# Second expert products in plain float32, all remaining expert splits on VectorE, and another order of the first transfers, in a decoder layer with conv, attention, state-space and 16 experts

## The chip, the core and the metric

The kernel runs on one core of a Trainium2 chip. A core has five engines with in-order instruction streams of their own: TensorE (PE; its weight loads are shown as PEld), VectorE (DVE), ScalarE (ACT), GpSimd (POOL) and SyncE (SP), which here only issues transfers. They meet through semaphores. The metric is the device time of one launch in microseconds (us).

## The reference

One layer over 1040 tokens (16 learned meta tokens and 1024 tokens of x) with a model width of 1024, all in float32. After the layer the meta rows are dropped.

```python
z = rms_norm(h, norm_mix_g)
cv_a, cv_g, q, k, v, f_lg, s_u = split(z @ w_in)
y = concat(conv(cv_a, cv_g),               # depthwise, 31 taps, layer norm, silu
           rms_norm(attention(q, k, v, f_lg)),
           rms_norm(s5_mixer(s_u, lam_re, lam_im, log_dt, ...)))   # 32 groups x 64 states
h = h + y @ w_out
t = rms_norm(h, norm_ffn_g)
# router: best of 4 groups, best 2 of its 4 experts -> gates[:, 16]
for e in range(16):
    out += gates[:, e:e+1] * ((silu(t @ w1[e]) * (t @ w3[e])) @ w2[e])   # 1024 -> 256 -> 1024
h = h + out
return rms_norm(h, final_norm_g)[16:]
```

`ssm_lam_re` and `ssm_lam_im` have shape (32, 64) and `ssm_log_dt` has shape (32): one number for each group and state, and one for each group.

## The kernel before, in words

**Split products.** Most matrix products are made of three TensorE passes in the type fp32r. An operand is split into a high part (ScalarE copies it into fp32r) and a low part (the rest, by a subtraction on VectorE or GpSimd). `mm3` (L283 to L289) then adds high times high (L287), high times low (L288) and low times high (L289) for each 128 rows of the contraction. A float32 operand that goes into a matmul unsplit is multiplied in plain float32; one pair of products of the state-space part does that already (L1946).

**Front.** Nine token tiles (the meta rows and eight of 128 tokens, called x0 to x7 here) are requested by `load_h` on SP into `hb`, which has three buffers. `norm_h` takes the mean square on ACT (L315), scales the tile on DVE (L320), turns it with eight TensorE transposes (L326), and splits it (ACT L328 high, DVE L329 low). `load_w` requests 128 columns of `w_in` (L344) and splits them (L346, L347). The first three column groups are multiplied chunk by chunk (400, 384 and 256 tokens): I call these chunks c0, c1 and c2. Each has three groups of 24 matmuls, so c0 to c2 are 216 matmuls. They need tiles meta to x2, x3 to x5, and x6 and x7.

**State-space parameters.** `ssm_tables.params` (L1638 on) reads lam_re, lam_im (L1675, L1676) and log_dt (L1678) straight into the layout of 128 partitions x 8, so that each element is a piece of a transfer by itself. A chain of small DVE instructions makes exponentials, sines and cosines from them. `build` makes tables on GpSimd and DVE: the W tables (1024 elements a partition, L1631 to L1636), and E by repeated doubling on GpSimd (8 to 512 elements wide). `kernel` turns W on TensorE (L1824) and multiplies it (L1831).

**Order of the work.** Up to the experts a scheduler orders the instructions of each engine at build time. In the expert part the order is written out by hand: a list ORDER of step names is walked once for each expert `e` (with `e - 1` and `e + 1` overlapped).

**Experts.** For each expert the rows routed to it come in one or two blocks of 128 tokens, gathered by GpSimd (L1239). The second block hangs on a branch. A block is turned on TensorE (L1249), split (ACT L1255, DVE L1256), multiplied with w1 and w3 (`first`: 8 x 3 matmuls of 512 columns), gated (ACT L1266, DVE L1268, L1269), turned again (L1275), split (`gate_turned`: ACT L1280, DVE L1281), and multiplied with w2 (`second`: for each of two halves 2 x 3 matmuls of 512 columns). The result is scaled by the gate and added to the rows in memory by an indirect transfer (L1292). The weights of an expert are three loads (`load`) of 128 x 2048 floats: q = 0 and 1 hold w1 and w3, q = 2 holds w2. Each is split in two halves by `split`: one ACT copy (L1327) and one subtraction (L1328) of 128x1024 each. The steps a0, a1, b0, b1 (q = 0, 1) give the subtraction to VectorE, the steps w0, w1 (q = 2) to GpSimd (VectorE for the last expert). The loads share six buffers `eraw`, and their high and low parts five buffers each. After the last gather, rows of the residual are read, added, normed and written out beside the last experts (`residuals`, `dense_in`, `dense_out`, `tick`). A loop for a third and later block of an expert stands behind it and is not entered with these inputs.

## Time and profile before

| | |
|---|---|
| time, median of 3 runs | 943.05 us (940.55 to 946.97) |
| the profiled execution's own time, and its span | 945.53 us, 943.8 us |
| mean granted TensorE clock in it (1 is full speed) | 0.916 |
| TensorE matmuls | 795.9 us busy, 84% of the span |
| VectorE | 723.5 us, 77% |
| ScalarE | 464.0 us, 49% |
| GpSimd | 415.7 us, 44% |
| transfers | 122.13 MB, 135 GB/s of main memory traffic over the span |

The busy tenths in 40 slices of 23.6 us say where an engine is full. TensorE starts at 0 and 5, has 9 in most slices up to the experts, 6 to 9 in the experts (slices 27 to 38) and 0 in the last. VectorE has 9 in the slices of the convolution and of the tail. A row of a view of groups gives the line, the engine, the operation, the tiles and shapes, the count, the busy time and the mean of one instruction, and then how long the engine stood idle just before such an instruction and what ended that. Because the engines work in order, an instruction that waits holds up all that stands behind it on its engine.

### The profile page before, as it was taken

Reading aid. Unit: us, or ns where it says so; the run is one execution under the profiler, and the core shown is the slowest. Engines: PE = TensorE matmul, PEld = TensorE weight load, DVE = VectorE, ACT = ScalarE, POOL = GpSimd, SP = SyncE. Lnnn points to the kernel's source line nnn. Section 1 sums busy time; section 2 is a strip of 40 time slices with the busy share of each in tenths; the row PEclk is TensorE's granted clock in tenths of the full one; section 3 lists DMA queues with packets and bytes.
Section 4 is the critical chain, followed back from the end, with each engine's and each line's share of the span. In section 5 each row is a group of like instructions: output and inputs, shape, how many; then the busy total and the mean of one; then the engine's idle time right before and its main releaser. Section 6 shows DMA issues by size and latency. Waiting matters only on the chain. (4 is left out here: it accounts for less than half of the span.)

```text
span 943.8 us, 15100 instructions
## 1 busy us (share of the span) xinstructions
PE 795.9 (84%) x5154; PEld 661.4 (70%) x5155; DVE 723.5 (77%) x1712; ACT 464.0 (49%) x803; POOL 415.7 (44%) x437
## 2 busy tenths in 40 slices
PE   0588898899999978989989999927899997998680
PEld 0488897698999956666668888825687775776560
DVE  3853997988858488998977657675779688798895
ACT  3332265325234275776764332415557476577662
POOL 0094995740000063656683001143456456456465
PEclk9999998899999986998978999958999999998795
DMA  5513125113220032011124341119788779879652
GB/s 124 158 46 93 39 63 114 31 26 101 53 90 24 1 113 79 24 69 40 43 100 139 112 134 68 67 46 351 264 269 263 247 195 276 263 219 295 234 205 98
DMA packets 92084, 122.13 MB, mean 129 GB/s; under 512 B 17931, under 2 KB 72986, under 8 KB 92000
## 3 DMA queue, kind: packets, MB, share of 16 engines
q1 hardware_dynamic: 84944, 101.98, 33.2%
q0 software_dynamic: 7056, 19.09, 7.9%
q8 instruction: 45, 0.74, 0.3%
q14 instruction: 39, 0.32, 0.1%
HBM read 101.16 MB, written 26.52 MB: 135 GB/s over the span
## 5 line engine op out<-in xcount | busy, mean ns | idle before, releaser
L287 PE MATMUL psum<-arena,arena 128*128 128x512 f32 (+5 forms) x848 | 309.2, 365 | 12.1 <-ACT arena L513 4.1
L288 PE MATMUL psum<-arena,arena 128*128 128x512 f32 (+5 forms) x848 | 303.1, 358 | 7.3 <-DVE arena L347 4.3
L289 PE MATMUL psum<-arena,arena 128*128 128x512 f32 (+5 forms) x848 | 302.0, 357 | 0.0
L287 PEld LDWEIGHTS psum<-arena,arena 128*128 128x128 f32 (+1 forms) x848 | 164.1, 194 | 33.7 <-issue 7.2
L288 PEld LDWEIGHTS psum<-arena,arena 128*128 128x128 f32 (+1 forms) x848 | 164.1, 194 | 23.5 <-DVE arena L347 4.5
L289 PEld LDWEIGHTS psum<-arena,arena 128*128 128x128 f32 (+1 forms) x848 | 163.5, 193 | 17.0 <-DVE arena L347 0.4
L1328 POOL TENSOR_TENSOR arena<-arena,arena 128x1024 fp32r<-128x1024 f32 x34 | 90.7, 2672 | 106.1 <-ACT arena L1327 90.4
L773 POOL TENSOR_TENSOR arena<-arena 128x512 f16<-128x512 f32 (+4 forms) x104 | 109.0, 1066 | 62.5 <-DVE arena L772 36.0
L1328 DVE TENSOR_TENSOR arena<-arena,arena 128x1024 fp32r<-128x1024 f32 x62 | 121.5, 1992 | 18.8 <-ACT arena L1327 18.7
L1327 ACT ACTIVATE arena<-arena 128x1024 fp32r<-128x1024 f32 x96 | 98.7, 1072 | 4.0 <-DMA arena<-in_exp_w_dram 2.9
L767 ACT ACTIVATE arena<-psum,arena 128x512 f32<-128x512 f32 (+4 forms) x112 | 63.8, 588 | 36.8 <-PE psum L763 15.9
L670 DVE CUSTOM_DVE_ANT_0 arena<-psum,arena 128x144 bf16<-128x144 f32 (+6 forms) x112 | 54.9, 501 | 22.3 <-PE psum L665 9.0
L1249 PE MATMUL psum<-arena 128*128 128x128 f32 x256 | 43.7, 302 | 32.3 <-DVE arena L1256 23.2
L780 PE MATMUL psum<-arena,arena 128*128 128x65 f16 (+3 forms) x1056 | 61.5, 206 | 7.9 <-DVE arena L741 3.4
L780 PEld LDWEIGHTS <-arena 128*128 128x128 f16 (+1 forms) x1056 | 47.8, 105 | 28.7 <-POOL arena L773 10.4
L1249 PEld LDWEIGHTS psum<-arena 128*128 128x128 f32 x256 | 33.1, 154 | 46.8 <-DVE arena L1256 28.7
L1255 ACT ACTIVATE arena<-psum 128x512 fp32r<-128x512 f32 x64 | 38.5, 601 | 43.1 <-PE psum L1249 43.1
L759 PE MATMUL psum<-arena 128*128 128x512 f32 (+4 forms) x112 | 52.3, 468 | 1.7 <-ACT arena L770 1.2
L665 PE MATMUL psum<-arena 128*128 128x144 f32 (+7 forms) x112 | 45.4, 411 | 7.9 <-DVE arena L670 7.8
L433 DVE SCALAR_TENSOR_TENSOR psum<-arena,psum 128x1024 f32<-128x1024 f32 x40 | 51.3, 1282 | 0.7
L819 POOL MEMSET arena<- 128x9 f16 x2 | 0.2, 166 | 115.6 <-PE psum L288 115.6
L443 POOL TENSOR_TENSOR arena<-arena 128x512 f32<-128x512 f32 x36 | 48.6, 1377 | 5.7 <-ACT arena L440 5.7
(315 smaller groups left out, 1479.4 us busy)
## 6 DMA issues: line engine op xcount, KB each, us to landing
arena<-in_exp_w_dram SPq DMA_DIRECT2D x64, 512.0 KB, 7.5
arena<-in_exp_w_dram SPq DMA_DIRECT2D x16, 1024.0 KB, 5.3
arena<-in_x_dram SPq DMA_DIRECT2D x16, 512.0 KB, 4.5
arena<-in_w_in_dram SPq DMA_DIRECT2D x14, 512.0 KB, 4.3
arena<-cr_d SPq DMA_DIRECT2D x8, 520.0 KB, 3.7
arena<-in_w_out_dram SPq DMA_DIRECT2D x8, 512.0 KB, 3.6
h_d<-arena SPq DMA_DIRECT2D x8, 512.0 KB, 3.0
t_d<-arena SPq DMA_DIRECT2D x8, 512.0 KB, 4.0
```

The source lines that it names most:

```text
L287: PE.matmul(out=acc, lhsT=lh[k], rhs=rh[k], start=(k == 0), stop=False)
L288: PE.matmul(out=acc, lhsT=lh[k], rhs=rl[k], start=False, stop=False)
L289: PE.matmul(out=acc, lhsT=ll[k], rhs=rh[k], start=False, stop=(k == n - 1))
L433: V.scalar_tensor_tensor(out=yc, in0=ub[:, m, w:w + NX], scalar=cwt[:, m, w:w + 1], in1=yc, op0=OP.mult, op1=OP.add)
L670: V.tensor_tensor_reduce(out=jk_b()[:, :b - a], in0=sp, in1=nrow[:, a:b], scale=1.0, scalar=-3.0e38, op0=OP.add, op1=OP.max, accum_out=mp[ ...
L759: PE.matmul(out=sp, lhsT=KS[:, k0:k0 + nk], rhs=QS[:, q0:q1], start=True, stop=False)
L767: S.activation(out=pt, in_=sp, func=AF.Exp, bias=bias)
L773: (V if cnt[0] % 5 in HV[h] else G).tensor_tensor(out=pl, in0=pt, in1=ph, op=OP.subtract)
L780: PE.matmul(out=po[:, i - i0, 0:v1 - v0], lhsT=w[:, qs], rhs=vb[:nk, j, v0:v1], start=(j == 0 and i == i0 and n == 0), stop=(j == i and n ...
L1249: PE.transpose(tp[:, k, :], xg[:, c:c + 128], ident)
L1327: S.activation(out=h[:, cs], in_=raw[:, cs], func=AF.Copy)
L1328: eng.tensor_tensor(out=l[:, cs], in0=raw[:, cs], in1=h[:, cs].bitcast(F32), op=OP.subtract)
```

## The change

- All nine token tiles get a buffer of their own (`hb` 9), and all are requested near the start of the program.
- lam_re, lam_im and log_dt are read as rows (8 partitions x 128, and 8 x 2), log_dt is repeated over 64 states by a DVE copy, three TensorE transposes turn them, and one DVE copy brings them from PSUM into place.
- `gate_turned` only copies (ACT), and `second` multiplies plain float32 operands: two matmuls for each half and no low parts. w2 is not split any more: the steps w0 and w1 are gone. w2 gets three buffers of its own (`ew2`), and its load for expert e + 3 is requested behind the second product of expert e. `eraw` goes from six to four buffers, and the high and low parts from five to four.

```diff
+    par = A.alloc("par", [3, 128], parts=8), A.alloc("par2", [2], parts=8)
-    hb = A.rot("h", [D], 3)
+    hb = A.rot("h", [D], 9)
...
     load_h(2)
+    load_h(3)
     norm_h(0, 2)
     wu = [load_w(2056, 128)]
-    load_h(3)
+    load_h(4)
     norm_h(2, 3)
     wu.append(load_w(2056 + 128, 128))
-    load_h(4)
+    load_h(5)
     norm_h(3, 4)
     wu.append(load_w(256, 128))
+    for i in range(6, 9):
+        load_h(i)
...
         if c == 0:
             for i in range(5, 8):
-                load_h(i)
                 norm_h(i - 1, i)
         if c == 1:
-            load_h(8)
...
-        raw = raw_b()
+        raw = raw_b() if q < 2 else w2_b()
...
-        order += [(e + 1, 1)] * (e + 1 < NE) + [(e, 2)] + [(e + 2, 0)] * (e + 2 < NE)
+        order += [(e + 1, 1)] * (e + 1 < NE) + [(e + 2, 0)] * (e + 2 < NE)
...
-    raw_b.more(3)
+    raw_b.more(1)
-    wh_b = A.rot("ewh", [2048], 5, F32R)
-    wl_b = A.rot("ewl", [2048], 5, F32R)
+    wh_b = A.rot("ewh", [2048], 4, F32R)
+    wl_b = A.rot("ewl", [2048], 4, F32R)
+    w2_b = A.rot("ew2", [2048], 3, flex=False)
...
     def gate_turned(tp):
-        ah, al = ah_b(), al_b()
-        S.activation(out=ah, in_=tp, func=AF.Copy, scale=0.5)
-        V.scalar_tensor_tensor(out=al, in0=tp, scalar=0.5, in1=ah.bitcast(F32), op0=OP.mult,
-                               op1=OP.subtract)
-        return ah, al
+        aa = aa_b()
+        S.activation(out=aa, in_=tp, func=AF.Copy, scale=0.5)
+        return aa
...
-        mm3(yp, [ah[:, k, :] for k in range(2)], [al[:, k, :] for k in range(2)],
-            [w2[0][:, k, cs] for k in range(2)], [w2[1][:, k, cs] for k in range(2)])
+        for k in range(2):
+            PE.matmul(out=yp, lhsT=aa[:, k, :], rhs=w2[:, k, hf * 512:hf * 512 + 512],
+                      start=(k == 0), stop=(k == 1))
...
+    def load2(e):
+        if e < NE:
+            w2s[e] = v2(load_raw(e, 2))
...
             for k in ([hf] if b == 0 else range(2)):
                 second(w2s[e], aa[e, b], yps[e, b, k], k)
+        if b:
+            load2(e + 3)
...
-        "w0": (lambda e: split(e, 2, 0, G if e + 1 < NE else V), 0),
-        "w1": (lambda e: split(e, 2, 1, G if e + 1 < NE else V), 0),
...
+        SY.dma_start(out=pr[:, 0, :], in_=dram(p["ssm_lam_re"], 0, [[128, 8], [1, 128]]))
+        SY.dma_start(out=pr[:, 1, :], in_=dram(p["ssm_lam_im"], 0, [[128, 8], [1, 128]]))
+        SY.dma_start(out=l2, in_=dram(p["ssm_log_dt"], 0, [[2, 8], [1, 2]]))
+        V.tensor_copy(out=pr[:, 2, :].rearrange("q (a s) -> q a s", a=2),
+                      in_=l2[:, :, None].to_broadcast([8, 2, 64]))
+        tp = self.bank("ss")[:, :24].rearrange("p (k q) -> p k q", q=8)
+        for k in range(3):
+            PE.transpose(tp[:, k, :], pr[:, k, :], self.ident[:8, :8])
         lr, li, ld = t8(), t8(), t8()
-        SY.dma_start(out=lr, in_=dram(p["ssm_lam_re"], 0, [[1, 128], [128, 8]]))
-        SY.dma_start(out=li, in_=dram(p["ssm_lam_im"], 0, [[1, 128], [128, 8]]))
-        for par in range(2):
-            SY.dma_start(out=ld[par * 64:par * 64 + 64], in_=dram(p["ssm_log_dt"], par, [[0, 64], [2, 8]]))
+        V.tensor_copy(out=self.sm[:, self.cnt - 3:self.cnt, :], in_=tp)
```

The change adds lines, so a line of the front stands at 1 to 4 higher numbers in the changed kernel, and one of the tables at 3 to 9 higher. Three places of the order that the diff alone does not tell follow.

First place: SP, whose transfers go out in this order, from its first weight load on. Before:

```order
L344 DMA arena_61<-in_w_in_dram 128x8x128 x2
L1675 DMA arena_61<-in_ssm_lam_re_dram 128x8x1
L1676 DMA arena_61<-in_ssm_lam_im_dram 128x8x1
L1678 DMA arena_61<-in_ssm_log_dt_dram 64x8x1 x2
L1681 DMA arena_61<-in_ssm_b_re_dram 128x8x16
L1681 DMA arena_61<-in_ssm_b_im_dram 128x8x16
L1926 DMA arena_865<-in_ssm_norm_g_dram 128x256
L310 DMA arena_61<-in_x_dram 128x1024
L344 DMA arena_61<-in_w_in_dram 128x8x128 x2
L310 DMA arena_61<-in_x_dram 128x1024
L344 DMA arena_61<-in_w_in_dram 128x8x128
L310 DMA arena_61<-in_x_dram 128x1024 x3
```

Of the change:

```order
L345 DMA arena_61<-in_w_in_dram 128x8x128
L311 DMA arena_61<-in_x_dram 128x1024
L345 DMA arena_61<-in_w_in_dram 128x8x128
L311 DMA arena_61<-in_x_dram 128x1024 x4
L413 DMA arena_61<-in_conv_w_dram 31x256
L416 DMA arena_61<-in_conv_b_dram 128x2x1
L1678 DMA arena_61<-in_ssm_lam_re_dram 8x128
L1679 DMA arena_61<-in_ssm_lam_im_dram 8x128
L1680 DMA arena_61<-in_ssm_log_dt_dram 8x2
L1690 DMA arena_61<-in_ssm_b_re_dram 128x8x16
L1690 DMA arena_61<-in_ssm_b_im_dram 128x8x16
L345 DMA arena_61<-in_w_in_dram 128x8x128 x2
```

The five element-wise loads (lam_re, lam_im, log_dt twice, and conv_b later) are one (conv_b), all token tiles stand ahead of it, and the third weight load stands behind b_re and b_im.

Second place: ACT in the front, from the copies of tile x0 on (rows L328 and L329 are the high parts of turned tiles, L346 and L347 those of weights, L315 and L316 mean squares). Before:

```order
L328 ACTIVATE arena_60<-psum 128x4x128
L346 ACTIVATE arena_81<-arena_61 128x1024
L328 ACTIVATE arena_60<-psum 128x4x128
L315 ACTIVATE arena_61<-arena_61 128x1024
L328 ACTIVATE arena_60<-psum 128x4x128 x3
L315 ACTIVATE arena_61<-arena_61 128x1024
L328 ACTIVATE arena_60<-psum 128x4x128
```

Of the change:

```order
L329 ACTIVATE arena_60<-psum 128x4x128
L347 ACTIVATE arena_81<-arena_61 128x1024
L329 ACTIVATE arena_60<-psum 128x4x128
L316 ACTIVATE arena_61<-arena_61 128x1024 x3
L329 ACTIVATE arena_60<-psum 128x4x128
L316 ACTIVATE arena_61<-arena_61 128x1024
L329 ACTIVATE arena_60<-psum 128x4x128 x2
L347 ACTIVATE arena_81<-arena_61 128x1024
L329 ACTIVATE arena_60<-psum 128x4x128 x2
L386 ACTIVATE arena_61<-psum 128x8x50 x2
```

The copy of the third weight (the second L347) now stands ahead of the copy of the second half of x2, which c0 needs.

Third place: GpSimd in one expert of the steady part, without its branches (L1292 and L1293 are the scatters, L1239 and L1243 the gathers). Before:

```order
L1239 DMA arena_61<-t_d,arena_61 128x1026
L1239 DMA arena_61<-t_d,arena_61 128x1026
L1328 TENSOR_TENSOR arena_82<-arena_61,arena_60 128x1024
L1292 DMA h_d<-arena_61 1024x1024
L1328 TENSOR_TENSOR arena_82<-arena_61,arena_60 128x1024
L1292 DMA h_d<-arena_61 1024x1024
```

Of the change:

```order
L1243 DMA arena_61<-t_d,arena_61 128x1026
L1243 DMA arena_61<-t_d,arena_61 128x1026
L1293 DMA h_d<-arena_61 1024x1024
L1293 DMA h_d<-arena_61 1024x1024
```

Only the transfers are left there.

## Rows read from the trace of the kernel before

**Rows 1.** Windows: start and end, length, busy of each engine, clock, DMA share, GB/s.

```profile
0.00:100.00 100.00, 61.78 (x340) 57.04 (x342) 52.40 (x228) 29.46 (x52) 39.76 (x141) 0.97 0.37 103
250.00:300.00 50.00, 50.00 (x328) 48.13 (x329) 35.33 (x142) 14.14 (x36) 0.00 (x0) 1.00 0.24 71
```

**Rows 2.** Timeline of the front: start us, duration us, engine, line, [idle before <-releaser].

```profile
9.60 2.31 SPq L1678 DMA_DIRECT2D arena<-in_ssm_log_dt_dram  x2
...
15.11 6.83 SPq L1926 DMA_DIRECT2D arena<-in_ssm_norm_g_dram  x1
...
22.15 0.17 DVE L1648 TENSOR_SCALAR arena<-arena 128x8 f32<-128x8 f32 x1 [9.28 <-DMA arena<-in_ssm_log_dt_dram]
...
27.09 1.06 ACT L315 ACTIVATE arena<-arena 128x1024 bf16<-128x1024 f32 x1 [14.03 <-DMA arena<-in_x_dram]
...
39.90 0.70 PE L288 MATMUL psum<-arena,arena 128*128 128x400 f32 x1 [0.77 <-DVE arena L329]
```

**Rows 3.** Windows of the front's transfers, columns as in rows 1.

```profile
2.00:10.00 8.00, 0.00 (x0) 0.00 (x0) 3.05 (x14) 5.00 (x8) 0.25 (x2) 1.00 1.01 309
12.00:20.00 8.00, 1.12 (x4) 0.71 (x4) 0.86 (x4) 1.06 (x2) 0.00 (x0) 1.00 0.05 0
20.00:24.00 4.00, 0.30 (x2) 0.30 (x3) 1.85 (x10) 0.00 (x0) 0.00 (x0) 1.00 0.58 64
```

**Rows 4.** Timeline, the tables and the end of chunk c2.

```profile
48.34 0.20 POOL L1631 TENSOR_TENSOR arena<-arena 128x8 f32<-128x8 f32 x1 [46.10 <-DVE arena L1646]
...
90.35 0.43 PE L289 MATMUL psum<-arena,arena 128*128 128x400 f32 x1
...
104.24 2.46 DVE L1633 TENSOR_TENSOR arena<-arena 128x1024 f32<-128x1024 f32 x1
```

**Rows 5.** Timeline of PE and PEld: a plain product, and steps of fp32r.

```profile
237.11 1.88 PE L1946 MATMUL psum<-arena 128*128 128x512 f32 x4
...
237.54 0.19 PEld L1946 LDWEIGHTS psum<-arena 128*128 128x128 f32 x1 [0.24 <-issue]
237.97 0.19 PEld L1946 LDWEIGHTS psum<-arena 128*128 128x128 f32 x1 [0.24 <-issue]
...
668.14 0.39 PE L287 MATMUL psum<-arena,arena 128*128 128x512 f32 x1
668.37 0.39 PE L288 MATMUL psum<-arena,arena 128*128 128x512 f32 x1
```

**Rows 6.** Groups: count, busy us, mean ns, idle before; L1281 from 640 us on.

```profile
L1328 POOL TENSOR_TENSOR arena<-arena,arena 128x1024 fp32r<-128x1024 f32 x34 | 90.7, 2672 | 106.1 <-ACT arena L1327 90.4
L1327 ACT ACTIVATE arena<-arena 128x1024 fp32r<-128x1024 f32 x96 | 98.7, 1072 | 4.0 <-DMA arena<-in_exp_w_dram 2.9
...
L1281 DVE SCALAR_TENSOR_TENSOR arena<-psum,arena 128x256 fp32r<-128x256 f32 x32 | 13.3, 416 | 5.8 <-ACT arena L1280 5.8
```

**Rows 7.** Windows: twelve experts, one of them, two of the last.

```profile
651.00:850.00 199.00, 179.82 (x844) 142.59 (x844) 163.72 (x229) 127.89 (x202) 107.27 (x55) 0.96 0.84 256
782.60:798.10 15.50, 12.01 (x56) 8.61 (x56) 11.79 (x18) 10.73 (x18) 10.54 (x7) 1.00 1.01 299
863.20:906.80 43.60, 34.54 (x135) 26.48 (x136) 38.55 (x77) 28.04 (x48) 23.68 (x13) 0.81 0.73 265
```

**Rows 8.** L1328 by itself from 640 us: ns min/median/max, then a pair.

```profile
L1328 DVE TENSOR_TENSOR arena<-arena,arena x60: 1206/1211/4794, 649.1 to 912.1; 128x1024 fp32r<-128x1024 f32 x60
...
794.60 4.12 DVE L1328 TENSOR_TENSOR arena<-arena,arena 128x1024 fp32r<-128x1024 f32 x1 [2.88 <-ACT arena L1327]
...
794.72 2.92 POOL L1328 TENSOR_TENSOR arena<-arena,arena 128x1024 fp32r<-128x1024 f32 x1
```

**Rows 9.** Waits from 640 us: engine line <- releaser, us in total, times, longest.

```profile
PE psum L1249 <- DVE arena L1256: 23.2, 12, 5.5
```

**Rows 10.** The page's groups: the same subtraction on VectorE in the whole span.

```profile
L1328 DVE TENSOR_TENSOR arena<-arena,arena 128x1024 fp32r<-128x1024 f32 x62 | 121.5, 1992 | 18.8 <-ACT arena L1327 18.7
```

**Rows 11.** Timeline of the last experts, GpSimd's last subtraction.

```profile
897.09 3.39 POOL L1328 TENSOR_TENSOR arena<-arena,arena 128x1024 fp32r<-128x1024 f32 x1
```

More of the change, by code (lines that the diff above doesn't have):

```diff
@@ L487 @@
     tabs = ssm_tables(nc, A, bank, dr, p, dram, ident)
-    tabs.params()
+    tabs.params(*par)
+    A.free("par", "par2")
     conv(0)
@@ L1229, in moe @@
     sg_b = A.rot("sg", [FF], 2, flex=False)
-    ah_b = A.rot("ah", [2, 128], 3, F32R)
-    al_b = A.rot("al", [2, 128], 3, F32R)
+    aa_b = A.rot("aa", [2, 128], 3, flex=False)
     yt_b = A.rot("yt", [D], 2, flex=False)
@@ L1308, in gate_of @@
         return g
-    def shaped(t, q):
-        return v4(t) if q < 2 else v2(t)
     xgs, xx, aa, gs = {}, {}, {}, {}
-    wts = {}
+    wts, w2s = {}, {}
     def refill():
@@ L1332, in weights @@
     def weights(e, q):
-        return [shaped(t, q) for t in wts.pop((e, q))]
+        return [v4(t) for t in wts.pop((e, q))]
+    def load2(e):
+        if e < NE:
+            w2s[e] = v2(load_raw(e, 2))
     for w, eng in ((order[0], G), (order[1], V), (order[2], G)):
@@ L1348, in moe @@
             tc.no_sync_barrier()
-            for t in raw_b.aps:
+            for t in raw_b.aps + w2_b.aps:
                 G.memset(t[:, 255:257], 0.0)
-            for _ in range(6):
+            for k in range(3):
                 refill()
+                load2(k)
+            refill()
     def come(b):
@@ L1395, in tick, with halves @@
         del later[:n]
-    def halves():
-        raw = raw_b()
+    def halves(b=raw_b):
+        raw = b()
         return [raw[:, 0:D], raw[:, D:2 * D]]
@@ L1437, in add @@
         sums(late, b)
-    hr, row, yts, hps, w13s, w2s, sgs, tps, yps = {}, {}, [None, None], {}, {}, {}, {}, {}, {}
+    hr, row, yts, hps, w13s, sgs, tps, yps = {}, {}, [None, None], {}, {}, {}, {}, {}
     def do_gather(e):
@@ L1473, in do_second @@
     def do_second(e, b, hf):
-        if (e, 2) in wts:
-            w2s[e] = weights(e, 2)
         for k in ([hf] if b == 0 else range(2)):
@@ L1545, in moe @@
         2: {"ga": lambda: prepare(2), "a1": lambda: last_in(4, 4, halves()),
-            "w1": lambda: row.update({14: halves()}),
+            "w1": lambda: row.update({14: halves(w2_b)}),
             "end": lambda: (tick(99), residuals(late + 2, row[14]),
@@ L1577, in moe @@
                 wt = []
-                for q in range(3):
+                for q in range(2):
                     raw, h, l = load(e, q), wh_b(), wl_b()
@@ L1581, in moe @@
                     V.tensor_tensor(out=l, in0=raw, in1=h.bitcast(F32), op=OP.subtract)
-                    wt.append([shaped(h, q), shaped(l, q)])
+                    wt.append([v4(h), v4(l)])
+                wt2 = v2(load(e, 2))
                 V.tensor_copy(out=ixd, in_=lst[:, bass.ds(e * 8 + b, 1)])
@@ L1590, in moe @@
                 hp = bank("h")
-                first(wt[:2], xx, hp)
+                first(wt, xx, hp)
                 aa = gate_turned(turn_gate(gate(hp)))
@@ L1594, in moe @@
                     yp = bank("y")
-                    second(wt[2], aa, yp, hf)
+                    second(wt2, aa, yp, hf)
                     V.tensor_scalar(out=yt[:, hf * 512:hf * 512 + 512], in0=yp, scalar1=g,
@@ L1636, in cmul, with params @@
         e2.tensor_tensor(out=oi, in0=oi, in1=t1, op=OP.add)
-    def params(self):
+    def params(self, pr, l2):
         nc, pm, p, dram, t8, cmul = self.nc, self.pm, self.p, self.dram, self.t8, self.cmul
@@ L1672, in exp_ @@
             return o
+        SY.dma_start(out=pr[:, 0, :], in_=dram(p["ssm_lam_re"], 0, [[128, 8], [1, 128]]))
[4 more added lines that the diff above has]
+        tp = self.bank("ss")[:, :24].rearrange("p (k q) -> p k q", q=8)
+        for k in range(3):
+            PE.transpose(tp[:, k, :], pr[:, k, :], self.ident[:8, :8])
         lr, li, ld = t8(), t8(), t8()
-        SY.dma_start(out=lr, in_=dram(p["ssm_lam_re"], 0, [[1, 128], [128, 8]]))
-        SY.dma_start(out=li, in_=dram(p["ssm_lam_im"], 0, [[1, 128], [128, 8]]))
-        for par in range(2):
-            SY.dma_start(out=ld[par * 64:par * 64 + 64], in_=dram(p["ssm_log_dt"], par, [[0, 64], [2, 8]]))
+        V.tensor_copy(out=self.sm[:, self.cnt - 3:self.cnt, :], in_=tp)
         B = [pm.tile([128, 8, 16], F32, name=f"B{r}") for r in range(2)]
```

2 lines of the change are left out of this document (removed).

## The prediction

> **What bounds the kernel now.** The granted clock and the windows by stage were read first, then the waits of each engine, and then the timeline of the two stages that the change touches, the front and the experts.
>
> The windows show two kinds of stretch. From 250 to 300 us TensorE is busy for 50.00 of 50 us [rows 1]: in the middle it is the bound, and an engine that feeds it earlier gains nothing there, but whatever TensorE starts earlier it also ends earlier. In the first 100 us it is busy for 61.78 us [rows 1], so 38 us are waits. That is the front. In the twelve experts from 651 to 850 us it is busy for 179.82 of 199 us [rows 7], and DVE for 163.72: TensorE is nearly the bound, with DVE close behind. In two of the last experts, 863 to 907, DVE is busy for 38.55 of 43.6 us and TensorE for 34.54 at a granted clock of 0.81 [rows 7]: there DVE leads.
>
> In the front the timeline is read for what each wait ended on. SP issues the two loads of log_dt at 9.60, a load of 128 KB behind them holds SP for 6.83 us from 15.11, and only then, at 22, comes the request for x2. DVE waits 9.28 us for log_dt, ACT 14.03 us for x2, and the first low product of c0 starts at 39.90 [rows 2]. The transfers explain it: from 2 to 10 us they run at 309 GB/s with a share of 1.01, and from 12 to 20 us they move nothing that shows, while the element-wise loads are under way [rows 3]. So TensorE waits for tiles that are not requested because the queue ahead of them is stuck, not because memory is full.
>
> In the experts the waits name what holds TensorE: its turns (L1249) wait 23.2 us in 12 waits for DVE's L1256 [rows 9], and L1256 stands behind the subtraction L1328 in DVE's order. That subtraction takes 1.21 us in the median and up to 4.79 us; 4.12 us is what it takes where GpSimd runs its own L1328 of 2.92 us at the same time [rows 8]. Over the whole span its mean is 1.99 us for 62 of them [rows 10], so about 62 x (1.99 - 1.21) = 48 us of DVE's time is this collision.
>
> **The change, part by part: the front** (SP's and ACT's order are the first and second place shown). All tiles are requested ahead of the small loads. Meta rows, x, the norm's row and two weights are 5.8 MB. At 309 GB/s [rows 3] they take 18.8 us, so they are in at about 21. The parameters are 24 rows instead of 3072 single elements and follow at once. b_re and b_im are unchanged, 128 KB, and ran at 64 GB/s [rows 3]: 2 us. The third weight, behind them, lands at about 26 (estimate from these rows).
>
> What is late next is that weight. In the new order ACT copies it (1.06 us) ahead of the second half of x2, and c0 needs that half. So c0 starts at about 28 to 29 instead of 39.90, 11 us earlier. The three turns of the parameters and the two copies are a few tenths of a us each, and lie in the wait for that weight: they cost nothing, and without this cover about 1 us.
>
> c1 needs x3 to x5, which waited for buffers before. They are there, and DVE's chain of small parameter instructions lies between their low parts. I put c1's start at 48 instead of 59 and its end at 62. c2 then meets the next late thing: DVE's order has the 1024-wide table instructions (3 us and 2.46 us [rows 4]) ahead of the low parts of x6 and x7, and the turns of the W table now stand between c1 and c2 on TensorE. The chain that feeds the tables began on GpSimd at 48.34 [rows 4], only after DVE had its sines; with log_dt landing at about 22 as before it begins at about 50 again. The copies it makes there take 6 to 7 us, DVE's three products 7 us, the low parts 3 us: c2 starts at about 69, and the projection behind it at about 80, with 3 us of W turns and products already done, where it stood at 90.35 [rows 4] with these still to come. That is 10 + 3 = 13 us; I take **-12 us**, since E on GpSimd now comes later and can hold DVE once. The bounds are -4 (TensorE waits at the W turns until 88, two thirds of the gain gone) and -18 (c2 does not wait for the tables). TensorE has no wait from 250 to 300 us [rows 1], so what it gains in front of that arrives whole behind it.
>
> **The experts: TensorE pays.** A block's second product was 12 fp32r matmuls of 512 columns, one each 0.23 us (668.14 to 668.37 [rows 5]): 2.76 us. It becomes four plain float32 ones. A plain one shows as two records; their weight loads are 0.43 us apart (237.54, 237.97 [rows 5]), so one takes 0.86 us and the block 3.44 us. That is +0.68 us for each of 22 blocks: **+15 us** of TensorE at full clock.
>
> The Trainium skill, "FP8 and Floating Point Precision", section "TensorE Precision Notes", says that true FP32 takes four passes through the array; against three passes of the split product that would be 4/3 of 2.76 us, 3.68 us for a block, and +20 us over 22 blocks. The case's own rows give 1.24 times instead of 4/3, and I take the rows; by the page the sum would come out 5 us higher.
>
> **DVE and GpSimd are relieved.** Gone are GpSimd's 30 subtractions of expert w2 (34 in all, mean 2.67 us, 90.7 us [rows 6]), 32 ACT copies of 1.07 us, and 32 DVE subtractions L1281 of 0.42 us (13.3 us [rows 6]). GpSimd then does nothing but transfers in the steady part, so DVE's remaining L1328 falls to 1.21 us, of which there are four for an expert: for an expert 4 x 0.78 + 0.42 = 3.5 us less on DVE. ACT is not a bound; its relief costs and gives nothing by itself.
>
> What that is worth: from 651 to 850 us, 199 - 180 = 19 us of TensorE's time is waits, and some of the busy time ran at half clock (mean 0.96). Five of the twelve experts there have two blocks, so 17 blocks add 17 x 0.68 = 11.6 us. At full clock with no wait at all the work is about 175 + 11.6 = 187 us: -12. If no wait goes it is +12. I take 193, **-6**, since most waits of L1249 end on DVE, but part of the others are on transfers (share 1.01 in the expert 782.6 to 798.1 [rows 7]) and stay.
>
> From 850 us DVE leads. Over four experts it loses two subtractions of the last w2, which fell to DVE there (4 us at the mean of 1.99 [rows 10]), eight L1281 (3.3 [rows 6]) and collisions (about 7), and GpSimd loses the 3.39 us L1328 [rows 11] that stands ahead of the residual rows' gathers. Of these 18 us I count half as on the path, 9, and take off 3 for TensorE's five blocks: **-6**, bounds -14 and +3. Behind 920 us nothing changes.
>
> The request for w2 comes behind the second product, three experts ahead, so two periods of some 15 us [rows 7] lie between the request and the use: this wait costs nothing. Four buffers instead of six for w1 and w3 hold two experts, as before.
>
> **Sum:** 945.5 - 12 - 6 - 6 = 921.5 us against the profiled execution, which is 2.5 us above the median of 943.05. Against the median: **919 us**.
>
> **Rivals.**
>
> *The experts give nothing.* TensorE is 90% busy there [rows 7] and gets 15 us more work; DVE's waits are only 23.2 us [rows 9] and part of them stays. Then only the front is gained: 943 - 12 = 931 us, and with 3 us of loss in the experts 934. For it: TensorE's share; against it: an expert with one block, such as 782.6 to 798.1 with TensorE busy for 12.01 of 15.5 us [rows 7], is not bound by TensorE. Chance 0.17.
>
> *The experts give all.* Every wait on DVE goes, -12 and -14, with the front: 943 - 38 = 905 us. Chance 0.10.
>
> *The wait moves within the front.* The third weight or the tables take the place of the tiles, the front gives 3 us, the experts 12: 928 us. For it: the tables' chain starts on GpSimd at the same 48 us and three things on TensorE now hang on it early. Against it: 0 GB/s for 8 us is a true hole. Chance 0.10.
>
> *Slower.* The plain product lies on TensorE itself, 15 us at full clock and more where the clock is half, and the collisions that go are not what L1256 waits for (its waits are for ACT's part or the gathered rows). It decides where less than 3 of the 19 us of waits go, with a front that gives 3: 943 + 12 + 3 - 3 = 955 us. For it: TensorE is the busiest engine of the stage. Against it: the pair at 794.6, where DVE is held for 2.9 us beyond its own 1.21. Chance 0.06.
>
> A page's rule bears on the collision: the Trainium skill, "SBUF — State Buffer", section "SBUF: two separate sides", calls the port pair of GpSimd and VectorE an exclusive lock, so the later one blocks whole. The pair at 794.6 and 794.72 agrees: DVE ends 1.08 us after GpSimd. By that rule the collisions would go to the last one, which is the rival that gives all.
>
> **Numbers.** The forecast has 0.52, the rivals 0.17, 0.10, 0.10 and 0.06; the other 0.05 is a change that comes to nothing, 937 to 948. The range leaves out half of the case that gives all, the slower one and the rest: 902 to 936 us. Runs of this kernel differ by some us, and 1% (9.4 us) is about what can be told from no change: faster means below 933.6. The forecast, the cases at 905 and 928, and about 0.10 of the 0.17 lie there: 0.82. Within 1%: 0.12. Slower: 0.06.
>
> **What would show it.** Front: the first low product of c0 at 28 to 30 us, c2 done at about 78, no stretch with 0 GB/s from 12 to 20. If c0 starts behind 34, the third weight was mis-sized; if the W turns wait for DVE's table instructions by 10 us or more, the tables were. Experts: L1328 on DVE at 1.21 us in the mean, plain matmuls 0.86 us apart, L1249's wait for L1256 below 8 us, the stretch from the first expert's gate to 13 gates later below 195 us. If those waits stay while L1328 is short, the forecast for the experts is wrong at its root.

## The result, and the profile after

The changed kernel takes 920.63 us in the median of four runs (917.61 to 925.5) against 944.67 us before: a ratio of 0.9754, 95% interval 0.9710 to 0.9798. Six more runs of it, beside those of the last experiment, gave 918.48 us and 0.9739 (0.9710 to 0.9768). The profiled execution took 920.6 us, its span is 918.9 us.

**Front.** Windows of the changed kernel, columns as in [rows 1]:

```profile
0.00:100.00 100.00, 77.76 (x444) 73.35 (x446) 64.08 (x246) 35.50 (x62) 51.73 (x138) 0.93 0.44 113
12.00:20.00 8.00, 2.92 (x13) 2.12 (x12) 7.43 (x21) 7.23 (x13) 0.11 (x1) 1.00 1.06 340
72.87:79.98 7.11, 7.00 (x32) 6.60 (x33) 1.95 (x2) 3.28 (x6) 7.11 (x14) 0.50 0.95 207
```

The hole of [rows 3] is gone: from 12 to 20 us the transfers run at 340 GB/s, where 0 showed. TensorE is busy for 77.76 of the first 100 us instead of 61.78 [rows 1].

The timeline of the same kernel, the instructions that answer to [rows 2] and [rows 4]:

```profile
21.42 0.21 DVE L1681 COPY arena<-arena 8x128 f32<-8x128 f32 x1 [0.84 <-DMA arena<-in_ssm_log_dt_dram]
...
24.06 1.05 ACT L347 ACTIVATE arena<-arena 128x1024 fp32r<-128x1024 f32 x1
25.50 0.54 PE L288 MATMUL psum<-arena,arena 128*128 128x400 f32 x1
...
47.35 0.20 POOL L1634 TENSOR_TENSOR arena<-arena 128x8 f32<-128x8 f32 x1 [14.24 <-DVE arena L1649]
...
53.96 1.23 DVE L1634 TENSOR_TENSOR arena<-arena 128x1024 f32<-128x1024 f32 x1 [0.21 <-POOL arena L1745]
...
61.06 0.39 PE L288 MATMUL psum<-arena,arena 128*128 128x256 f32 x1 [0.71 <-DVE arena L330]
...
72.87 2.34 PE L1833 MATMUL psum<-arena 128*128 128x128 f32 x8 [3.38 <-POOL arena L1639]
...
79.98 0.68 PE L287 MATMUL psum<-arena,arena 128*128 128x400 f32 x1
```

DVE waits 0.84 us for log_dt, where it waited 9.28. The third weight is copied at 24.06, the first low product of c0 runs at 25.50 instead of 39.90, c2's at 61.06, and the projection behind the chunks begins at 79.98. GpSimd's table chain starts at 47.35, hardly earlier than the 48.34 of [rows 4], as forecast. Ahead of the projection TensorE waits 3.38 us for GpSimd and then does the W work in 7.1 us at a granted clock of 0.50 (the 1.2 GHz level; the last window above).

The row at 90.35 in [rows 4] is not the projection's first product, nor the end of c2, but the projection's first product with the weight's low part. Its first product of all ran here in the kernel before:

```profile
87.34 0.45 PE L287 MATMUL psum<-arena,arena 128*128 128x400 f32 x1 [1.03 <-ACT arena L346]
```

So the projection begins 7.4 us earlier (87.34 to 79.98), and not 10.

**Experts.** First the windows of the first twelve experts (from the gate of the first expert to that of the thirteenth) and of all that is behind them, then the waits, the subtraction, and the plain products and their weight loads:

```profile
643.96:834.30 190.34, 183.40 (x780) 128.23 (x780) 115.99 (x205) 105.41 (x178) 47.14 (x30) 0.97 0.86 264
834.30:918.90 84.60, 53.96 (x200) 32.81 (x200) 62.21 (x131) 45.94 (x80) 35.98 (x21) 0.86 0.64 230
```

```profile
PE psum L1253 <- DVE arena L1260: 3.8, 2, 3.6
```

```profile
L1326 DVE TENSOR_TENSOR arena<-arena,arena 128x1024 fp32r<-128x1024 f32 x58 | 69.0, 1221 | 28.4 <-ACT arena L1325 28.4
```

```profile
675.65 0.19 PEld L1289 LDWEIGHTS psum<-arena 128*128 128x128 f32 x1 [0.24 <-issue]
676.08 0.19 PEld L1289 LDWEIGHTS psum<-arena 128*128 128x128 f32 x1 [0.24 <-issue]
```

The stretch went from 199.0 to 190.3 us, what is behind it from 93.8 (850.0 to 943.8) to 84.6. DVE's subtraction has a mean of 1.221 us (1.99 in [rows 10]), the turns wait 3.8 us for DVE instead of 23.2 [rows 9], DVE is busy for 116 us of the twelve experts instead of 164, and TensorE for 183.4 of 190.3, 96%: by this window it is the bound there, which `half_second` below tries. The plain products stand 0.43 us apart for each of their two records, 0.86 us for one.

So the parts are, by these two executions: the front and all up to the first turn of the experts -8.6 us (640.5 to 631.9), from there to the end -16.3.

### The profile page after: what moved, and what is told of

Read it like the earlier page. It is cut to its first block, busy times and chain, and to the rows that moved or that the text cites. A ratio compares the mean times of both kernels' runs of the same rounds, so it can differ in the third digit from the quotient of the medians.

```text
span 918.9 us, 14826 instructions
## 1 busy us (share of the span) xinstructions
PE 806.2 (88%) x5069; PEld 643.7 (70%) x5070; DVE 662.4 (72%) x1680; ACT 432.9 (47%) x771; POOL 343.7 (37%) x408
## 5 line engine op out<-in xcount | busy, mean ns | idle before, releaser
L287 PE MATMUL psum<-arena,arena 128*128 128x512 f32 (+5 forms) x760 | 268.5, 354 | 7.6 <-DVE arena L599 5.8
L289 PE MATMUL psum<-arena,arena 128*128 128x512 f32 (+5 forms) x760 | 263.1, 347 | 2.7 <-DVE arena L348 1.9
L288 PE MATMUL psum<-arena,arena 128*128 128x512 f32 (+5 forms) x760 | 263.6, 347 | 1.0 <-DVE arena L330 1.0
L287 PEld LDWEIGHTS psum<-arena,arena 128*128 128x128 f32 (+1 forms) x760 | 145.5, 192 | 22.3 <-DVE arena L599 6.3
L289 PEld LDWEIGHTS psum<-arena,arena 128*128 128x128 f32 (+1 forms) x760 | 144.7, 190 | 15.6 <-DVE arena L348 2.2
L288 PEld LDWEIGHTS psum<-arena,arena 128*128 128x128 f32 (+1 forms) x760 | 145.5, 191 | 12.7 <-DVE arena L330 1.4
L776 POOL TENSOR_TENSOR arena<-arena 128x512 f16<-128x512 f32 (+4 forms) x104 | 114.3, 1116 | 62.2 <-DVE arena L775 41.6
L1326 DVE TENSOR_TENSOR arena<-arena,arena 128x1024 fp32r<-128x1024 f32 x60 | 71.4, 1221 | 28.5 <-ACT arena L1325 28.4
L1293 POOL DMA_INDIRECT h_d<-arena x17 | 34.4, 2024 | 137.6 <-DVE arena L1260 69.7
L1325 ACT ACTIVATE arena<-arena 128x1024 fp32r<-128x1024 f32 x64 | 66.1, 1071 | 8.0 <-DMA arena<-in_exp_w_dram 4.8
L1289 PE MATMUL psum<-arena 128*128 128x512 f32 x128 | 59.8, 604 | 2.3 <-PEq L1455 0.9
L1253 PEld LDWEIGHTS psum<-arena 128*128 128x128 f32 x256 | 32.6, 151 | 39.9 <-issue 16.8
L1260 DVE TENSOR_TENSOR arena<-psum,arena 128x512 fp32r<-128x512 f32 x64 | 43.8, 685 | 17.8 <-ACT arena L1259 17.6
L1253 PE MATMUL psum<-arena 128*128 128x128 f32 x256 | 40.3, 294 | 16.9 <-DMA arena<-t_d,arena 11.5
```

Of the source, the lines that this page charges most:

```text
L287: PE.matmul(out=acc, lhsT=lh[k], rhs=rh[k], start=(k == 0), stop=False)
L288: PE.matmul(out=acc, lhsT=lh[k], rhs=rl[k], start=False, stop=False)
L289: PE.matmul(out=acc, lhsT=ll[k], rhs=rh[k], start=False, stop=(k == n - 1))
L776: (V if cnt[0] % 5 in HV[h] else G).tensor_tensor(out=pl, in0=pt, in1=ph, op=OP.subtract)
L1253: PE.transpose(tp[:, k, :], xg[:, c:c + 128], ident)
L1289: PE.matmul(out=yp, lhsT=aa[:, k, :], rhs=w2[:, k, hf * 512:hf * 512 + 512], start=(k == 0), stop=(k == 1))
```

## The experiments

All comparisons are with the kernel before on the same chip.

**The two parts apart.** `front_only` is the kernel before with the front's lines of the diff (tiles and parameters), `experts_only` with all the others.

> The kernel before with the changed front alone (tiles first, parameters as rows); the experts are those of before. Theory A (front and experts gain apart, and the middle gives back what the trace of the changed kernel shows: 20 us ahead behind the state-space products, 8.6 us ahead at the experts' first turn): 8 to 10 us less than before, about 935 us. Rival (the give-back between is an accident of one execution and the gain of the front arrives whole): 20 us less, 925. Second rival (the 8.6 us are lost again in old experts that wait for transfers): 943.

Measured: 930.9 us, ratio 0.9839 (0.9778 to 0.9899), so -15 us (10 to 21).

> The kernel before with the changed experts alone (plain second products, w2 unsplit, remaining splits on VectorE); the front is that of before. Theory A (gains are apart; from the first turn to the end the changed kernel was 16 us shorter): 16 us less than before, about 928 us. Rival (the experts' gain is part of the front's, since the scheduler's order changed all over): 938 or more. The prediction had 12 us: 932.

Measured: 930.3 us, ratio 0.9834 (0.9785 to 0.9883), -16 us (11 to 20). Neither interval reaches 1, and each part works without the other. Their sum would be 0.967; the whole has 0.974 to 0.975. The 6 to 8 us that the whole lacks are within what the two intervals, of some 5 us either way each, leave to chance.

**Who was in whose way.** Three kernels around the collision of [rows 8]. `split_all_v` takes `front_only` and moves two steps:

```diff
-        "w0": (lambda e: split(e, 2, 0, G if e + 1 < NE else V), 0),
-        "w1": (lambda e: split(e, 2, 1, G if e + 1 < NE else V), 0),
+        "w0": (lambda e: split(e, 2, 0, V), 0),
+        "w1": (lambda e: split(e, 2, 1, V), 0),
```

> The changed front, the experts of before with split second products, but the subtractions of w2 (steps w0 and w1) on VectorE instead of GpSimd. Theory A (what slowed the experts was the collision of the two subtractions): VectorE gets 2 x 1.21 us more for an expert and loses 4 x 0.78 us of collisions, TensorE has 0.68 us less for a block than in the changed kernel; most of the 16 us stays, 922 to 928. Rival (it is the amount of split work, wherever it is done, that counts): no better than the changed front alone, 935 or more.

Measured: 916.18 us, ratio 0.9691 (0.9643 to 0.9738). VectorE does 30 more subtractions than in the kernel before, and the time falls by 15 us beside `front_only`. With the split second products of before it isn't slower than the changed kernel. Its groups (from 615 us on) and its windows for the twelve experts and for the rest:

```profile
L1331 DVE TENSOR_TENSOR arena<-arena,arena 128x1024 fp32r<-128x1024 f32 x92 | 114.9, 1285 | 15.9 <-ACT arena L1330 15.1
```

```profile
652.67:835.47 182.80, 173.85 (x844) 139.55 (x844) 149.03 (x253) 127.18 (x202) 51.08 (x30) 0.98 0.90 277
835.47:926.90 91.43, 54.46 (x224) 40.91 (x224) 73.88 (x147) 53.89 (x88) 39.22 (x21) 0.81 0.62 215
```

VectorE has 92 subtractions in 114.9 us, where 62 took 121.5 before [rows 10]: 30 more in less time. The twelve experts take 182.8 us, 7.5 less than in the changed kernel, and the rest 91.4, 6.8 more; its granted clock in the rest was 0.81, that of the changed kernel 0.86, and how much of the 6.8 us is the clock isn't shown.

`spare_splits` goes the other way. It is the changed kernel, and each step w0, w1 makes a copy and a subtraction of w2 whose results nothing uses:

```diff
+    def spare(e, a, eng):
+        h, l, raw = dh_b(), dl_b(), w2s[e][:, a, :]
+        S.activation(out=h, in_=raw, func=AF.Copy)
+        eng.tensor_tensor(out=l, in0=raw, in1=h.bitcast(F32), op=OP.subtract)
...
+        "w0": (lambda e: spare(e, 0, G if e + 1 < NE else V), 0),
+        "w1": (lambda e: spare(e, 1, G if e + 1 < NE else V), 0),
```

> The changed kernel with the copies and subtractions of w2 put back on ScalarE and GpSimd (for the last expert on VectorE), their results used by nothing. TensorE's work is that of the changed kernel. Theory A (collision): VectorE's L1326 goes back to 2 us in the mean, the waits of the turns for VectorE come back, and since the plain products stay it is slower than the changed front alone: 934 to 945. Rival (what helped is that the second product no longer needs split operands, not that GpSimd is idle): within 3 us of the changed kernel, 918 to 924.

Measured: 934.94 us, ratio 0.9929 (0.9887 to 0.9970). It isn't faster than `front_only` (930.9): all of the experts' gain is gone. A pair of its timeline, and its group:

```profile
709.42 2.96 POOL L1338 TENSOR_TENSOR arena<-arena,arena 128x1024 fp32r<-128x1024 f32 x1
710.25 3.23 DVE L1328 TENSOR_TENSOR arena<-arena,arena 128x1024 fp32r<-128x1024 f32 x1 [0.55 <-ACT arena L1327]
```

```profile
L1328 DVE TENSOR_TENSOR arena<-arena,arena 128x1024 fp32r<-128x1024 f32 x58 | 102.2, 1785 | 21.7 <-ACT arena L1327 19.1 <-ACT arena L1504 2.4
```

GpSimd ends at 712.38, DVE at 713.48, 1.1 us behind it: nearly the whole of DVE's instruction, 1.23 us when alone, came after GpSimd's. The other pairs of this trace and of the kernel before, taken one by one, say the same: in all 32 in which DVE's record begins between 0.73 us ahead of GpSimd's and GpSimd's end, DVE ends 1.08 to 1.10 us behind GpSimd; where it begins 0.9 us or more ahead, DVE ends first.

`spare_memset` keeps GpSimd as long busy at the same places, with an operation that reads nothing:

```diff
-        eng.tensor_tensor(out=l, in0=raw, in1=h.bitcast(F32), op=OP.subtract)
+        if eng is G:
+            for _ in range(3):
+                G.memset(l, 0.0)
+        else:
+            eng.tensor_tensor(out=l, in0=raw, in1=h.bitcast(F32), op=OP.subtract)
```

> The kernel spare_splits with GpSimd's two subtractions for an expert replaced by three memsets each of 128x1024 (about 0.9 us each): GpSimd is as long busy in front of its gathers and scatters, and ScalarE makes the same spare copies, but GpSimd reads no operand. Theory A (VectorE was held by GpSimd's reads): VectorE's L1326 is 1.22 us again and the time is that of the changed kernel, 918 to 925. Rival (GpSimd's work delays its own transfers, or any of its work holds VectorE): 930 to 940, as with the subtractions.

Measured: 919.13 us, ratio 0.9736 (0.9666 to 0.9807). The same place in its timeline:

```profile
708.31 3.56 POOL L1340 MEMSET arena<- 128x1024 f32 x3
709.16 1.23 DVE L1328 TENSOR_TENSOR arena<-arena,arena 128x1024 fp32r<-128x1024 f32 x1 [0.55 <-ACT arena L1327]
```

DVE starts in the middle of GpSimd's memsets and takes its 1.23 us, and each of its subtractions that overlaps a memset in this trace takes 1.22 to 1.25. The windows of the twelve experts, of `spare_splits` and then of `spare_memset`:

```profile
637.68:838.22 200.54, 187.28 (x780) 128.13 (x780) 147.34 (x205) 128.81 (x203) 108.50 (x55) 0.97 0.81 253
```

```profile
640.21:831.36 191.15, 183.57 (x780) 128.49 (x780) 117.08 (x205) 128.10 (x203) 108.05 (x97) 0.97 0.86 266
```

GpSimd and ScalarE are as long busy in both, but the same 205 instructions of VectorE take 147 us beside subtractions and 117 beside memsets. So neither GpSimd's busy time nor ScalarE's spare copies cost anything that can be told; what cost some 15 us is that GpSimd *read operands* while DVE wanted to. One thing more differs: the memsets don't wait for ScalarE's copies, for which GpSimd's subtractions waited 32.6 us in `spare_splits`. What that wait alone costs wasn't tried; VectorE's 30 us are not part of it. The rule of the Trainium skill, "SBUF — State Buffer", section "SBUF: two separate sides" (a lock on the shared port pair between GpSimd and a VectorE operation with two SBUF inputs, only against a GpSimd operation that reads SBUF) says just that, and here both halves of it show: 3.23 us against the reader, 1.23 against the memset. The same section of the Trainium skill gives the ports to the one that starts first; in these traces a record of DVE that begins up to 0.73 us ahead (0.12 in the pair of [rows 8]) still loses, so the start of a record doesn't say who has the ports.

**What the plain product costs.** `half_second` leaves the second half of the contraction out:

```diff
-        for k in range(2):
-            PE.matmul(out=yp, lhsT=aa[:, k, :], rhs=w2[:, k, hf * 512:hf * 512 + 512],
-                      start=(k == 0), stop=(k == 1))
+        PE.matmul(out=yp, lhsT=aa[:, 0, :], rhs=w2[:, 0, hf * 512:hf * 512 + 512],
+                  start=True, stop=True)
```

> The changed kernel with only the first of the two plain products of each half (the second half of the contraction with w2 is left out): TensorE has 1.72 us less for a block, 38 us for 22 blocks, and nothing else changes. Theory A (with VectorE free, TensorE is the bound of the experts and pays the plain products in full): 20 to 30 us less than the changed kernel, 892 to 901 us, with the transfers as the next bound. Rival (the transfers, whose share is 0.8 to 1.0 there, or VectorE already are the bound): less than 8 us, 913 to 921.

Measured: 902.12 us, ratio 0.9563 (0.9495 to 0.9631), 18 us below the changed kernel: between the two. About half of the 38 us comes back. Its windows for the twelve experts and for the rest:

```profile
643.81:815.79 171.98, 158.84 (x716) 115.69 (x716) 116.56 (x205) 104.46 (x179) 42.75 (x30) 0.96 0.94 292
815.79:906.10 90.31, 50.62 (x176) 31.79 (x176) 64.30 (x131) 46.14 (x80) 36.47 (x21) 0.75 0.61 217
```

The twelve experts take 172.0 us instead of 190.3: 18 of the 29 us (17 blocks of 1.72 us) that TensorE has less to do there. So TensorE held most of that stretch; what holds the rest isn't shown, but the share of the transfers rose from 0.86 to 0.94 while TensorE's fell to 92%. Behind them nothing comes back: 90.3 us against 84.6, at a granted clock of 0.75 against 0.86.

**Which half of the front.** `tiles_experts` is the changed kernel with the parameters read element by element as before (the last hunk of the diff undone, and the two small buffers for the rows).

> The changed kernel with the state-space parameters read element by element as before; all token tiles still go out first. Theory A (the tiles were late because they stood behind the element-wise loads): c0 starts as early, at about 25 us, but log_dt lands at 35 to 40, the tables and the W turns are late by 12 us or more and TensorE waits for them between c1 and c2; of the front's 15 us some 5 stay: 925 to 931. Rival (the order of the tiles is all, the rows nothing, since the tables have slack): 918 to 923.

Measured: 930.97 us, ratio 0.9871 (0.9802 to 0.9940), 10 us above the changed kernel. Beside `experts_only` (0.9834), which has neither half of the front, the tiles alone bring nothing that can be told. The time is at the edge of what theory A said; its way there was wrong. A window and the timeline:

```profile
20.00:28.00 8.00, 0.90 (x5) 0.43 (x3) 0.50 (x5) 1.96 (x4) 0.11 (x1) 1.00 0.05 0
```

```profile
31.93 0.17 DVE L1649 TENSOR_SCALAR arena<-arena 128x8 f32<-128x8 f32 x1 [11.00 <-DMA arena<-in_ssm_log_dt_dram]
33.42 1.06 ACT L346 ACTIVATE arena<-arena 128x1024 fp32r<-128x1024 f32 x1 [11.46 <-DMA arena<-in_w_in_dram]
...
37.72 0.68 PE L288 MATMUL psum<-arena,arena 128*128 128x400 f32 x1
```

The hole of 0 GB/s is back, now from 20 to 28 us, behind the tiles: it goes with the element-wise loads. The tiles are there, but DVE's order has the first parameter instruction among the tiles' low parts, and it waits 11 us; ACT waits 11.46 us for the third weight, which is stuck behind the element-wise loads. c0's first low product runs at 37.72, only 2 us earlier than before. The order of the tiles needs the rows to gain; the rows alone were not tried, so how much of the front's gain they would bring without that order stays open.

**A better split of the work.** By these readings TensorE mostly bounds the twelve experts, where a split second product is 0.68 us cheaper for a block, and VectorE the last ones. `hybrid13` has experts 0 to 12 split on VectorE and 13 to 15 plain.

> The changed front; experts 0 to 12 with split second products and the subtractions of w2 on VectorE, experts 13 to 15 with plain second products and w2 unsplit; w2 in two buffers, its next load behind the split. Theory A (TensorE is the bound of the steady part, where a split second product is 0.68 us cheaper, and VectorE that of the last experts, where no split is cheaper): below both the changed kernel (920) and split_all_v (916): 908 to 914. Rival (two buffers for w2, or transfers as the bound, take it back): 916 or more.

Measured: 909.73 us, ratio 0.966 (0.9591 to 0.9729). Its two buffers for w2 are one too few at the end: by the order of its steps, rows of the residual are written over w2 of expert 14 ahead of its product, so that product is made with other numbers than the weights, and the time is only a hint. `hybrid13b` and `hybrid14` take a third w2 buffer in exchange for the fifth pair of buffers for high and low parts:

> The changed front; experts 0 to 12 with split second products and the subtractions of w2 on VectorE, experts 13 to 15 plain; w2 in three buffers as in the changed kernel, four buffers each for high and low parts. Theory A (TensorE bounds the steady part, VectorE the last experts): as hybrid13, 906 to 913. Rival (the fifth pair of buffers is needed, since a split waits for the second product before it): 914 to 918.

> As hybrid13b, but expert 13 too with a split second product; only experts 14 and 15 are plain. Theory A (VectorE leads from expert 13 on): 1 to 4 us more than hybrid13b. Rival (TensorE still leads in expert 13): 1 us less.

Measured: 1001.64 us (ratio 1.0605, 1.0549 to 1.0660) and 1006.05 us (1.0651, 1.0584 to 1.0718). `hybrid13b` missed its forecast by far. By the order of the steps five pairs are in use at the step a0, so with four a split writes over weights that are still to be multiplied, and some products are made with the wrong weights. The waits of `hybrid13b` show the queue that goes with it: TensorE's L287 waits 54.1 us for ScalarE's L1340, a split, and L1340 waits 87.1 us for TensorE's L289. These two kernels say nothing on where the plain product should begin.

`split_v_last_plain` is `split_all_v` with the last expert alone plain: its w2 has a buffer to itself by then.

```diff
+        aa[e, b] = (gate_turned if e < last else gate_whole)(tps[e, b])
...
+                (second if e < last else second_whole)(w2s[e], aa[e, b], yps[e, b, k], k)
...
+        "w0": (lambda e: e < last and split(e, 2, 0, V), 0),
+        "w1": (lambda e: e < last and split(e, 2, 1, V), 0),
```

> split_all_v with one edit: the last expert's second product is plain and its w2 unsplit (its load has a buffer to itself by then). Theory A (TensorE bounds the steady part, VectorE the last experts, where split_all_v took 91.4 us from the 13th gate to the end and the changed kernel 84.6): 2 to 4 us less than split_all_v, 912 to 915 us, and 5 us or more below the changed kernel in the same job. Rival (the tail hangs on the norm's chain and transfers, not on these 3.3 us of VectorE): the same as split_all_v.

> The changed kernel once more, on the same chip as split_v_last_plain, to compare the two: 918 to 924 us.

Measured in one job: 913.83 us, ratio 0.9682 (0.9652 to 0.9713), and the changed kernel 918.48 us, 0.9739 (0.9710 to 0.9768). Its windows:

```profile
639.34:822.38 183.04, 173.46 (x844) 139.43 (x844) 149.12 (x253) 127.17 (x202) 51.04 (x30) 0.98 0.90 277
822.38:908.70 86.32, 52.42 (x216) 35.76 (x216) 70.16 (x143) 51.49 (x86) 37.72 (x21) 0.87 0.64 228
```

It has the 183 us of `split_all_v` in the twelve experts and 86.3 us behind them, near the changed kernel's 84.6. It is 5 us faster than the changed kernel in the medians; the intervals just touch. Against `split_all_v` itself (0.9643 to 0.9738) the 2 us can't be told.

**Where part of the front's gain went.** TensorE's milestones in the profiled executions, in us against the kernel before:

| TensorE's | after | front_only | spare_splits | changed_again | split_v_last_plain | split_all_v | experts_only | tiles_experts |
|---|---|---|---|---|---|---|---|---|
| first plain state-space product (L1946 before) | -19.6 | -20.9 | -20.5 | -21.1 | -18.4 | -18.8 | -3.0 | +0.5 |
| first score of the attention (L759) | -16.0 | -17.7 | -17.0 | -19.6 | -14.9 | -15.3 | -3.0 | 0.0 |
| last score (L759) | -14.6 | -19.0 | -21.8 | -16.4 | -18.3 | -6.0 | +2.9 | -3.1 |
| first turn behind it (L906) | -11.0 | -12.7 | -15.5 | -12.8 | -13.5 | +0.1 | +2.8 | +1.9 |
| first turn of the experts (L1249) | -8.6 | -11.6 | -14.8 | -10.5 | -12.0 | +1.3 | +3.8 | +4.1 |

About 20 us are gained by the state-space products. At the experts 9 to 15 are left, but none in the execution of `split_all_v` that was profiled. Each kernel with the new front loses 1 to 4 us between the first two rows and 3.6 to 6.3 us between the third and fourth, where `experts_only`, with the front of before, loses nothing (0 and 0.1). `tiles_experts`, which gains nothing ahead, loses 5.0 there too, which speaks for the order of the tiles, and not the rows, as the origin of that loss.

What VectorE does in that stretch can be read. It subtracts two operands there (L910 before, L913 after), the first three times between GpSimd's instructions in the kernel before, and in the changed kernel beside five of GpSimd's that read two operands too. First the kernel before, then the changed one:

```profile
498.65 0.42 DVE L910 TENSOR_TENSOR arena<-arena,arena 128x256 fp32r<-128x256 f32 x1 [1.63 <-PE psum L759]
```

```profile
480.47 6.61 POOL L776 TENSOR_TENSOR arena<-arena 128x512 f16<-128x512 f32 x5
483.96 3.41 DVE L913 TENSOR_TENSOR arena<-arena,arena 128x256 fp32r<-128x256 f32 x3 [0.43 <-PE psum L762]
```

From the last score to the first turn, seven of them take 2.8 us before and eight take 6.5 us after, while VectorE is busy for 9.5 of 10.4 us. So the collision of the experts stands here too; in the changed kernel it is some 3.2 us beyond the 0.42 us of each, near the loss of 3.6. That it is the cause is argued: no run took it out, and in `front_only`, where eight take 5.2 us and the loss is 6.3, it covers only a part.

In the attention itself (second to third row) the executions go from 5 us less to 9 us more than the kernel before, and the longest has the lowest granted clock of TensorE. Here the windows of the kernel before, and then of the execution of `split_all_v` that took 928.67 us in all, where its other four took 915.81 to 918.38:

```profile
330.00:505.00 175.00, 155.63 (x1566) 111.16 (x1565) 152.96 (x381) 121.06 (x216) 110.13 (x106) 0.84 0.19 63
```

```profile
315.50:505.00 189.50, 169.60 (x1565) 119.75 (x1563) 152.57 (x381) 121.21 (x216) 116.16 (x129) 0.77 0.20 67
```

Nearly the same instructions, a mean granted clock of 0.84 and 0.77 of full speed, 175.0 and 189.5 us. What costs the 1 to 4 us between the first two rows wasn't tried and stays open.

## Why the prediction was right, and where its steps were not

The forecast was 919 us; 920.6 and 918.5 were measured. Both mechanisms were named rightly, the stuck queue and the collision. That the number is so near is luck: of the front's gain more came than was said and more was lost again behind it, the experts gave more than was said, and these errors cancelled.

- **The bound of the front** was read rightly: the hole went with the element-wise loads, and it came back behind the tiles in `tiles_experts`. This run adds that without the rows the tiles alone bring nothing, which the sum had not split. The 3072 elements are right: there are 16 groups of 64 states, not 32 as the text on the reference says, so 1024 elements in each of lam_re and lam_im, and log_dt read 64 times over.
- **The terms of the front** were too small. c0 came at 25.5 instead of 28 to 29, since the third weight was there at about 24. c2 came at 61 instead of 69: the tables' chain began at 47.35 and not at 50, and the first two 1024-wide table instructions on DVE took 1.23 us each. The 3 us of the forecast are from the old trace, in which GpSimd ran such an instruction of its own (3.03 us) at that moment: the same collision as in the experts, and it was in the trace of before to be seen.
- **The projection** came at 79.98, where 80 was forecast, by luck: c2 was 8 us early, but the W work took 7.1 us at half clock where 3 were put, behind a wait of 3.4 us for GpSimd. The 10 us of the sum compared it with a row that is not its first (90.35); like for like it is 7.4, and a part of what comes on top is the W work done ahead. At the state-space products the gain is 20 us, not 12.
- **"The gain arrives whole"** is the step that failed. A saturated stretch from 250 to 300 us says only that TensorE holds that stretch. Behind it, at the end of the attention, VectorE was busy for 9.5 of 10.4 us, the order of the instructions had changed there too, and 6 to 11 us of the 20 were lost by the experts (all of it in one execution). The -12 of the sum was in the end within the interval of `front_only` (-10 to -21), by this loss.
- **TensorE's price** was right to the record: 0.86 us for a plain product, 3.44 us for a block. The estimate drawn from the four passes of true FP32 in the Trainium skill ("FP8 and Floating Point Precision", section "TensorE Precision Notes"), four thirds or 3.68 us, is not seen.
- **The experts** were put at -6 and -6 and measured -8.7 and -9.2. DVE's 1.21 us, the end of the waits for DVE and a stretch below 195 us came as written. The mechanism, the collision, is shown by `split_all_v`, `spare_splits` and `spare_memset`. What was short is the size: of the waits for DVE, of which a part was to stay, nearly all went (23.2 us to 3.8), so that TensorE is 96% busy.
- **The rivals.** That the experts give nothing, or lose, is refuted by `experts_only`. That they give all (-12 and -14) didn't come either: the -18 of the two windows lie between the -12 of the forecast and the -26 of this rival, nearer to the forecast. That the wait moves within the front is refuted.
- What the prediction did not see is that the plain product wasn't needed for any of this: `split_all_v` gains as much with the old products: the gain is in GpSimd's reads that are gone and not in the work saved.

## What to carry to other kernels

Before an operation with two operands from on-chip memory goes to an idle GpSimd, look in the trace at what VectorE's own such operations take while it runs: here GpSimd's 90.7 us of subtractions cost VectorE some 48 us (an estimate, 62 times the 0.78 us between the mean of 1.99 and the 1.21 us alone), and doing all of it on VectorE was faster. Look for loads of single elements ahead of the loads that start the work: here reading them as rows and asking for the tiles first gained together, and the order alone gained nothing. A gain at the start is worth what is left of it at the end of each stage with another bound, so follow it by milestones through the stages instead of passing it on whole.

## What was not expected of the hardware

- The same VectorE subtraction takes 1.23 us beside GpSimd memsets and 3.23 us beside a GpSimd subtraction. It ends 1.1 us after that one whether its own record begins 0.7 us ahead of GpSimd's or 1.2 us behind.
- The attention, with nearly the same instructions, took 175.0 us at a mean granted clock of 0.84 in the kernel before and 189.5 us at 0.77 in an execution of `split_all_v`; two executions with one and the same front differ by 3 to 4 us at the experts (`experts_only` against the kernel before). So a single profiled execution tells a part's gain to some us only.
- 3072 single elements (lam_re, lam_im, log_dt) held the first queue so long that no bytes showed for 8 us; as 24 rows they cost 0.84 us of waiting.
